# A two-block transformer on one core: seven-product pairs from the third pair of feed-forward tiles, sums one pair sooner

## The chip, the cores and the metric

One core of a Trainium2 chip runs the whole program in one launch. The metric is the device time of that launch in microseconds, the median of several runs. The engines are TensorE (PE, matmuls; PEld is its loading of weights), VectorE (DVE), ScalarE (ACT), GpSimd (POOL) and SyncE (SP, which issues most DMAs).

## The reference

Two blocks are applied to 512 tokens of width 1024, all in float32. The first is a hybrid of stick-breaking attention and a state-space scan. The second is: feed-forward part 1, a mixer (retention, multiscale pooling, gates), feed-forward part 2, a last norm. The change touches both feed-forward parts, which compute

```python
def swiglu_ffn(x, w_in, w_out):
    gate, up = jnp.split(x @ w_in, 2, axis=-1)
    return (jax.nn.silu(gate) * up) @ w_out
h = h + FFN_RES_WEIGHT * swiglu_ffn(rmsnorm(h, norm_ffn1[l]), ffn1_w_in[l], ffn1_w_out[l])
```

with 1024 inputs, an inner width of 2816 (`w_in` is 1024 x 5632, gate and up side by side) and a residual weight of one half.

## The kernel before, in words

Activations lie transposed: features on the 128 partitions, the 512 tokens along the free dimension, so an activation of width 1024 is 8 tiles of 128x512. To get float32 accuracy every operand is split into a rounded high part and the remainder (`split`, lines 111 to 118: ACT casts the high part, DVE subtracts). A product then takes three matmuls, high by high, high by low, low by high (`mm3`, lines with L102).

The inner width of 2816 is 22 tiles of 128, done in two halves of `FH` = 11. One step of the loop over `f` is a **pair**: the gate tile f and the up tile f. The result goes through Silu and the product of the two into `aa`. After each half come the eight output tiles.

There are two ways to do a pair. The **dense** one (f < `SF`, lines 1027 to 1048) takes for each of gate and up 8 blocks of weights by three matmuls of 512 columns, 48 matmuls. Its weights are loaded by SP (L131), cast by ACT (L137), and the low part is made by DVE (L139). The **seven-product** one (`strassen`, lines 976 to 1004) treats the pair as a 2x2 block product: inputs 0 to 3 and 4 to 7 (`xs`) by the two halves of the tokens, against gate and up weights. Seven products of 4 blocks by three matmuls of 256 columns, 84 matmuls (L959), are accumulated in the PSUM tiles `de`, `al`, `ga`. The order on PE is: `de` (opened ahead, before the pair before it is finished, by `open_pair`), then `al`, `ga`, `al`, `ga`, `al`, then the `de` of the next pair, then `al`. The second product into `al` follows a copy of the first out of it (ACT, L981). Besides the products it needs

- sums and differences of the activations, `T`, made once in each feed-forward part by four calls of `sums` (L902 to L905 on DVE, 128x256 each, then two splits: ACT L111, DVE L117). They read `xt`, the unsplit inputs. Every one of the four is needed by the second product (`ga`) of the first such pair;
- sums and differences of the weights, made for each pair by four calls of `prep`: part 0 splits the first loaded block (128x1024), parts 1 and 2 make two sums each (L939, L940, L943, L944 on DVE) and split them, part 3 casts half a block (ACT L111, L113) and gets its remainder by an accumulating DMA on POOL (L951). The raw blocks are loaded by `raws` (SP, L922).

In the first feed-forward part, `norm1` (called behind the last matmul of f=0) computes the norm's factors on DVE and POOL (L274 to L1105), broadcasts them by PE (`pb`), and rescales the eight residual tiles in place on DVE (L1110), which SP then writes to memory. In the second part `norm2` only makes one factor. The factor `Rb` is applied to the gate product on DVE (L1046), then Silu on ACT (L1047), the product with up on DVE (L1048) and the split into `aa`.

Order of work: on PE it is the order of the program, written out by hand. On the other engines the framework fixes an order ahead of the run, by its own planning. Working tiles (T before its split, the sums S, g, up, squares) come from one pool of 16 slots (`wk`), split activations from one of 54, weights' high parts from 4 slots (`wh`), low parts from 5 (`wl`), raw weights from 4 (`wr`), and PSUM tiles from 8.

In the kernel before, `SF` is 3: f = 0, 1, 2 are dense, the sums are made during f=1 (two) and f=2 (two), and the preparation of pair 3 during the up half of f=2.

Of the kernel before, what the change touches and what calls it, by code (L numbers as in the profile page):

```python
# [26 lines left out]
SLOTS = (54, 16, 4)  # L27
AHEAD = 3

SF = 3  # L30

PSH = (0, 1, 3, 5)
WARM = (12, 10, 4, 6, 6, 6)
# [20 lines left out]
def program(tc, A, out):  # L54
# [26 lines left out]
    def k_(dt=F32, name="k", shape=(P, S)):  # L81
        return wk.tile(list(shape), dt, tag="k", name=nm(name))
# [10 lines left out]
    def ps_(name="ps"):  # L93
        return pp.tile([P, S], F32, tag="p", name=nm(name))
# [9 lines left out]
    def mm3(o, w, x, start, stop):  # L104
        mm(o, w[0], x[0], start, False)
        mm(o, w[0], x[1], False, False)
        mm(o, w[1], x[0], False, stop)

    def cp(o, i, scale=None):
        if scale is None:  # L110
            ACT.copy(o, i)  # L111
        else:
            ACT.activation(o, i, AF.Copy, scale=scale)  # L113
# [6 lines left out]
    def split_into(h, l, src, scale=None):  # L120
        cp(h, src, scale)
        return lo(l, src, h, scale)
# [765 lines left out]
    def ffn(xs, xt, win, wout, norm, gnext, last=False, each=None):  # L888
# [7 lines left out]
        T = []  # L896

        def sums(k):

            t1, t2 = xt[k], xt[k + 4]  # L900
            u, v = k_(F32, "T"), k_(F32, "T")
            DVE.tensor_sub(u[:, lh], t1[:, rh], t1[:, lh])  # L902
            DVE.tensor_sub(u[:, rh], t2[:, rh], u[:, lh])
            DVE.tensor_sub(v[:, lh], t2[:, rh], t1[:, rh])
            DVE.tensor_sub(v[:, rh], t2[:, lh], u[:, rh])  # L905
            T.append((split(u, name="T"), split(v, name="T")))
# [11 lines left out]
        def raws(f):  # L918
            raw[f] = []
            for n in range(2):  # L920
                raw[f].append(wr.tile([P, 1024], F32, tag="wr", name=nm("wr")))
                SP.dma_start(raw[f][n], win[2 * f + n])  # L922

        def pair_of_tiles():
            return wh.tile([P, 1024], F32R, tag="wh", name=nm("wh")), wl.tile([P, 1024], F32R, tag="wl", name=nm("wl"))

        def quarter(i):
            return slice(512 * i, 512 * i + 512)

        def prep(f, part):  # L930
            r1, r2 = raw[f][:2]
            q0, q1 = quarter(0), quarter(1)
            h, l = pair_of_tiles()
            if part == 0:
                split_into(h, l, r1)
            elif part < 3:
                s, t = k_(F32, "S"), k_(F32, "S")
                if part == 1:
                    DVE.tensor_add(s, r2[:, q0], r2[:, q1])  # L939
                    DVE.tensor_sub(t, s, r1[:, q0])  # L940
                    raw[f].append(t)
                else:
                    DVE.tensor_sub(s, r1[:, q0], r2[:, q0])  # L943
                    DVE.tensor_sub(t, r1[:, q1], raw[f][2])  # L944
                for q, u in ((q0, s), (q1, t)):
                    split_into(h[:, q], l[:, q], u)
            else:

                cp(h[:, q0], r2[:, q1])
                cp(l[:, q0], r2[:, q1], -1.0)  # L950
                POOL.dma_start(l[:, q0], win[2 * f + 1, :, 512:1024], accum_op=ALU.add)  # L951
            ops.setdefault(f, []).append((h, l))
# [11 lines left out]
        def open_pair(f):  # L964
            pend[f] = ps_("de")
            product(pend[f], f, 0, 1, X(4, lh), True)
# [9 lines left out]
        def strassen(f, nf, aa, between):  # L976

            de, al, ga = pend.pop(f), ps_("al"), ps_("ga")
            g, v = k_(F32, "g"), k_(F32, "up")
            product(al, f, 0, 0, X(0, lh), True)  # L980
            ACT.copy(g[:, lh], al[:, lh])  # L981
            DVE.tensor_add(g[:, lh], de[:, lh], g[:, lh])
            if nf is not None:
                prep(nf, 0)
            product(ga, f, 1, 0, TT(0, lh), True)
            ACT.copy(v[:, rh], ga[:, lh])
            product(al, f, 1, 1, TT(0, rh), False)
            ACT.copy(g[:, rh], al[:, lh])
            if nf is not None:
                prep(nf, 1)  # L990
            product(ga, f, 2, 1, X(4, rh), False)
            DVE.tensor_add(g[:, rh], ga[:, lh], g[:, rh])
            product(al, f, 2, 0, TT(1, lh), False)
            order = DVE.tensor_add(v[:, rh], al[:, lh], v[:, rh])
            if nf is not None:
                prep(nf, 2)
                open_pair(nf)
            else:
                between()
            product(al, f, 3, 0, TT(1, rh), False)  # L1000
            finish(g, (al[:, lh], v[:, rh]), aa, order)
            if nf is not None:
                prep(nf, 3)
            ops.pop(f), raw.pop(f)

        for half in range(2):
            aa = []
            pos = []

            def opening():  # L1010

                pos.append(ps_("mp"))
                for k in range(2):
                    mm3(pos[0], so.next(), aa[k], k == 0, False)

            for f in range(half * FH, half * FH + FH):
                if f >= SF:
                    end = f == half * FH + FH - 1
                    if not end and f + 1 not in raw:
                        raws(f + 1)  # L1020
                    if end:
                        so.load(so.i)
                    strassen(f, None if end else f + 1, aa, opening)
                    if not end and f + 2 < half * FH + FH:
                        raws(f + 2)
                    continue
                pg, pu = ps_("mp"), ps_("mp")
                for n, ps in enumerate((pg, pu)):
                    for k in range(KD):
                        mm3(ps, si.next(), xs[k], k == 0, k == KD - 1)  # L1030
                        if each is not None and f == n == 0:
                            each(k)
                        if f == 0 and n == 1 and k in (2, 7):
                            norm(k // 7)
                        if f > 0 and n == 0 and k in (1, 5) and len(T) < 4:
                            sums(len(T))
                        if f == SF - 1 and n == 1 and k in (0, 2):
                            if k == 0:
                                raws(SF)
                            prep(SF, k // 2)  # L1040
                g = k_(F32, "g")
                if f == SF - 1:
                    prep(SF, 2)
                    open_pair(SF)
                    prep(SF, 3)
                DVE.tensor_mul(g, pg, ff["Rb"])  # L1046
                ACT.activation(g, g, AF.Silu)  # L1047
                DVE.tensor_mul(g, g, pu)  # L1048
                aa.append(split(g, name="aa"))
            for m in range(8):  # L1050
                if last and half == 1 and m == 6:
                    for i in (6, 7):
                        res[i] = a(F32, "res")
                        SP.dma_start(res[i], resd[i])
                    return aa, so
                xr = a(F32, "res") if last and half == 1 else tbl()
                SP.dma_start(xr, resd[m])
                k0 = 0 if m else 2
                ps = ps_("mp") if m else pos[0]
                for k in range(k0, FH):  # L1060
                    mm3(ps, so.next(), aa[k], k == 0, k == FH - 1)
                    if half == 0 and m == 7 and k in (0, 3, 4, 10):
                        if k == 0:
                            raws(FH)
                        else:
                            prep(FH, {3: 0, 4: 1, 10: 2}[k])
                if half == 0 and m == 7:
                    open_pair(FH)
                    prep(FH, 3)
                t = k_(F32, "t")  # L1070
                DVE.scalar_tensor_tensor(t, ps, 0.5, ff["Rb"], op0=ALU.mult, op1=ALU.mult)
                DVE.tensor_add(xr, xr, t)
                if half == 0:
                    SP.dma_start(resd[m], xr)
                    continue
                if gnext is not None:
                    nxt.append(split(xr, V(gnext, m), name="xs"))
                    SP.dma_start(resd[m], xr)
                else:
                    res[m] = xr  # L1080
                ff["ssq"] = accum(ff["ssq"], square(xr), DVE if m >= (4 if last else 6) else POOL)
# [451 lines left out]
```

## Time and profile before

| | us |
|---|---|
| median of 3 runs | 1715.0 (1714.86 to 1717.87) |
| the profiled execution | 1715.66 |
| its span | 1714.0 |
| PE busy | 1693.9 (99%) |
| DVE busy | 1112.6 (65%) |
| ACT busy | 807.9 (47%) |
| POOL busy | 221.0 (13%) |
| mean granted clock of PE | 0.992 |

The span runs from the first to the last instruction; the execution's time has a little around it. Rows of a timeline read: start, duration, engine, line of the kernel, operation, output tile and input tiles, count, and in brackets how long the engine had waited for nothing else and which instruction released it. A duration holds a part that overlaps with the next instruction, so the cost of one in a full queue is the distance from its start to the next start. In the chain of waits, each row is a stretch of the chain that ended last: start, length, what ran, how many. The first feed-forward part begins at about 515 us of the span, the second at about 1353.

### The profile page before, as it was taken

What the parts mean: (1) busy time and instruction counts of PE and PEld (TensorE: products, weight loads), DVE (VectorE), ACT (ScalarE), POOL (GpSimd) and SP (SyncE); (2) the same over time, 40 slices, a digit from 0 to 9 for tenths busy, and PEclk for the clock granted to TensorE, in tenths of its full rate; (3) what the DMA queues carried; (4) which work ended last, traced back from release to release, by engine and by line L of the source; (5) the groups of instructions that cost most, each with busy time, mean ns of one, the idle gap of its engine ahead of it and who ended that gap; (6) DMA issues with size and microseconds to landing.
All of it is one profiled execution on the core that took longest, in us unless ns stands there. A gap on an engine that the chain in (4) does not pass through costs nothing.

```text
span 1714.0 us, 24768 instructions
## 1 busy us (share of the span) xinstructions
PE 1693.9 (99%) x9488; PEld 1482.5 (86%) x9488; DVE 1112.6 (65%) x1757; ACT 807.9 (47%) x1344; POOL 221.0 (13%) x292
## 2 busy tenths in 40 slices
PE   9999899999999999999999999999999999999998
PEld 7898678888888998999888888888888899889987
DVE  7846953777957984798544636763544589559953
ACT  3555544777745661466333333332433466336642
POOL 0002202555400100000100000220000100000001
PEclk9999989999999999999999999999999999999999
DMA  9345448989563455445442322233333434544441
GB/s 327 106 127 187 137 128 220 215 192 210 146 153 107 125 155 164 129 125 155 164 150 91 88 91 86 80 99 97 93 95 129 158 93 124 166 129 137 124 166 50
DMA packets 84059, 236.36 MB, mean 138 GB/s; under 512 B 10018, under 2 KB 10338, under 8 KB 83940
## 3 DMA queue, kind: packets, MB, share of 16 engines
q1 hardware_dynamic: 74580, 210.66, 38.7%
q0 software_dynamic: 9360, 24.12, 8.2%
q8 instruction: 74, 1.21, 0.3%
q14 instruction: 45, 0.37, 0.1%
HBM read 207.44 MB, written 14.71 MB: 130 GB/s over the span
## 4 chain that ended last, share of the span: by engine, by line
PE 88%; DVE 3%; DMA 3%; issue 2%; ACT 2%; POOL 1%; SPq 0%; DVEq 0%; POOLq 0%; ACTq 0%
PE mp L102 53%; PE al L959 12%; PE mb L102 7%; PE ga L959 6%; PE de L959 3%; DMA wa<-in_adagt 1%; PE z L102 1%; PE sc L102 1%; PE po L102 1%; PE ro L102 1%; PE pw L772 1%; DMA wr<-in_wst 1%; DMA tb<-acd 1%; ACT tb L651 1%; ACT wh L137 0%
## 5 line engine op out<-in xcount | busy, mean ns | idle before, releaser
L137 ACT CAST wh<-wr 128x1024 fp32r<-128x1024 f32 (+3 forms) x212 | 217.6, 1030 | 463.7 <-PE mp L102 260.5
L139 DVE TENSOR_TENSOR wl<-wr,wh 128x1024 fp32r<-128x1024 f32 (+3 forms) x185 | 220.4, 1193 | 161.7 <-ACT wh L137 158.6
L102 PE MATMUL mp<-xsh,wh 128*128 128x512 f32 x416 | 164.6, 396 | 0.0
L102 PE MATMUL mp<-xsh,wl 128*128 128x512 f32 x416 | 162.2, 390 | 0.0
L102 PE MATMUL mp<-xsl,wh 128*128 128x512 f32 x416 | 162.0, 389 | 0.0
L111 ACT CAST wh<-S 128x512 fp32r<-128x512 f32 x152 | 93.7, 618 | 116.3 <-DVE S L943 59.2
L102 PE MATMUL mp<-aah,wh 128*128 128x512 f32 (+1 forms) x374 | 141.3, 378 | 0.0
L102 PE MATMUL mp<-aal,wh 128*128 128x512 f32 (+1 forms) x374 | 140.9, 377 | 0.0
L102 PE MATMUL mp<-aah,wl 128*128 128x512 f32 (+1 forms) x374 | 140.8, 376 | 0.0
L959 PE MATMUL al<-Th,wh 128*128 128x256 f32 x456 | 130.3, 286 | 2.3 <-ACT g L981 1.8
L959 PE MATMUL al<-Th,wl 128*128 128x256 f32 x456 | 129.0, 283 | 0.0
L959 PE MATMUL al<-Tl,wh 128*128 128x256 f32 x456 | 129.0, 283 | 0.0
L102 PE MATMUL mp<-hxh,wh 128*128 128x512 f32 x288 | 110.6, 407 | 2.0 <-ACT hxh L412 2.0
L102 PE MATMUL mp<-hxh,wl 128*128 128x512 f32 x288 | 107.0, 394 | 0.0
L102 PE MATMUL mp<-hxl,wh 128*128 128x512 f32 x288 | 106.7, 393 | 0.0
L117 DVE TENSOR_TENSOR wl<-S,wh 128x512 fp32r<-128x512 f32 x152 | 103.4, 684 | 0.2
L102 PEld LDWEIGHTS mp<-xsh,wl 128*128 128x128 f32 x416 | 78.0, 188 | 16.6
L102 PEld LDWEIGHTS mp<-xsh,wh 128*128 128x128 f32 x416 | 78.2, 188 | 15.7 <-issue 0.5
L102 PEld LDWEIGHTS mp<-xsl,wh 128*128 128x128 f32 x416 | 78.2, 188 | 15.6 <-issue 0.5
L959 PEld LDWEIGHTS al<-Th,wh 128*128 128x128 f32 x456 | 87.3, 192 | 4.2 <-ACT g L981 3.5
L959 PEld LDWEIGHTS al<-Tl,wh 128*128 128x128 f32 x456 | 87.4, 192 | 0.2
L959 PEld LDWEIGHTS al<-Th,wl 128*128 128x128 f32 x456 | 87.4, 192 | 0.0
(367 smaller groups left out, 4409.5 us busy)
## 6 DMA issues: line engine op xcount, KB each, us to landing
wr<-in_f1i SPq DMA_DIRECT2D x44, 512.0 KB, 3.9
wr<-in_f2i SPq DMA_DIRECT2D x44, 512.0 KB, 3.9
wr<-in_w2g SPq DMA_DIRECT2D x24, 512.0 KB, 3.5
wr<-in_f1o SPq DMA_DIRECT2D x22, 512.0 KB, 3.6
wr<-in_f2o SPq DMA_DIRECT2D x22, 512.0 KB, 3.6
tb<-res SPq DMA_DIRECT2D x32, 256.0 KB, 2.7
wr<-in_w2qk SPq DMA_DIRECT2D x16, 512.0 KB, 3.5
res<-res SPq DMA_DIRECT2D x24, 256.0 KB, 4.1
```

Of the source, the lines that this page charges most:

```text
L102: PE.matmul(o, l, r, start=start, stop=stop)
L111: ACT.copy(o, i)
L117: return DVE.tensor_sub(l, src, h.bitcast(F32))
L137: ACT.copy(h[:, :n], r[:, :n])
L139: DVE.tensor_sub(l[:, :n], r[:, :n], h[:, :n].bitcast(F32))
L651: ACT.activation(t[:, h, :], t[:, h, :], AF.Exp, bias=nac[:, hc : hc + 1])
L772: PE.transpose(pt[:, cc : cc + P], w[qb][:, kb * P : kb * P + P], ident)
L959: PE.matmul(o[:, lh], wk_[p], x[k][q], start=start and k == 0 and n == 0, stop=k == 3 and n == 2, skip_group_check=True)
```

## The change

`SF` becomes 2, so pair f=2 is done by seven products in both feed-forward parts, and the steps that lead up to the first such pair move one pair ahead. Of the four sums the first is called in the up half of f=0 behind the sixth block (k=5, ahead of the norm's call at k=7), the other three in the gate half of f=1 (k = 0, 3, 6). The loads of pair 2's raw blocks and the first two parts of its preparation are called in the up half of f=1, now at k = 0 and 3 in place of 0 and 2; the third and fourth part and `open_pair` follow behind f=1.

```diff
-SF = 3
+SF = 2
...
-                        if f > 0 and n == 0 and k in (1, 5) and len(T) < 4:
+                        if (f, n, k) in ((0, 1, 5), (1, 0, 0), (1, 0, 3), (1, 0, 6)):
                             sums(len(T))
-                        if f == SF - 1 and n == 1 and k in (0, 2):
+                        if f == SF - 1 and n == 1 and k in (0, 3):
                             if k == 0:
                                 raws(SF)
-                            prep(SF, k // 2)
+                            prep(SF, k // 3)
```

## The prediction

> **What bounds the kernel now.** I read the page first, then the chain of waits around both transitions from dense to seven-product pairs, then VectorE's (DVE's) and ScalarE's (ACT's) timelines there. The page says that TensorE (PE) is the bound.
>
> ```profile
> span 1714.0 us, 24768 instructions
> PE 1693.9 (99%) x9488; PEld 1482.5 (86%) x9488; DVE 1112.6 (65%) x1757; ACT 807.9 (47%) x1344; POOL 221.0 (13%) x292
> ```
>
> With PE at 99% a change counts only if it shortens PE's own work or the few places where PE waits. The chain of waits of the first feed-forward part (FFN 1) shows the two kinds of pair and such a place:
>
> ```profile
> 534.25 21.81 PE mp L102 x96
> 556.07 1.43 PE de L959 x12
> ...
> 561.83 1.69 PE al L959 x12
> ...
> 566.40 1.44 PE de L959 x12
> ...
> 572.52 1.69 PE al L959 x12
> ...
> 577.10 1.44 PE de L959 x12
> ...
> 587.18 1.44 PE de L959 x12
> ```
>
> Two dense pairs (f=1, 2) take 21.81 us, so 10.90 each; a seven-product pair in steady state takes 10.08 (577.10 to 587.18), 1.44 a product. The first one (f=3) is late: from its opening product `de` to the next `de` lie six products, 8.64 us, but 566.40 - 556.07 = 10.33. PE lost 1.69 there, and 577.10 - 566.40 - 10.08 = 0.62 in the next pair.
>
> What is late at 561.83, from the timelines of ACT and PE:
>
> ```profile
> 558.90 1.05 ACT L111 CAST wh<-wr 128x1024 fp32r<-128x1024 f32 x1 [0.85 <-ACT wh L111]
> ...
> 560.37 0.63 ACT L113 ACTIVATE wl<-wr 128x512 fp32r<-128x512 f32 x1
> 560.91 0.61 ACT L1047 ACTIVATE g<-g 128x512 f32<-128x512 f32 x1
> 561.43 0.35 ACT L981 COPY g<-al 128x256 f32<-128x256 f32 x1
> 561.83 0.38 PE L959 MATMUL al<-Th,wh 128*128 128x256 f32 x1 [1.45 <-ACT g L981]
> ```
>
> The third product writes `al` again, so it waits for ACT's copy out of `al` (L981). That copy stands in ACT's queue behind the Silu (L1047) of the last dense pair, and that waits for DVE's L1046. DVE is what is late:
>
> ```profile
> 526.98 0.16 DVE L274 TENSOR_SCALAR R1t<-pc 128x4 f32<-128x4 f32 x1 [8.65 <-PE pc L1091]
> ...
> 531.39 1.22 DVE L139 TENSOR_TENSOR wl<-wr,wh 128x1024 fp32r<-128x1024 f32 x1
> 533.46 1.23 DVE L139 TENSOR_TENSOR wl<-wr,wh 128x1024 fp32r<-128x1024 f32 x1 [0.85 <-ACT wh L137]
> 534.61 5.35 DVE L1110 SCALAR_TENSOR_TENSOR res<-res,vec,pb 128x512 f32<-128x512 f32 x8
> 539.87 0.68 DVE L1046 TENSOR_TENSOR g<-mp,tb 128x512 f32<-128x512 f32 x1
> 540.47 0.41 DVE L902 TENSOR_TENSOR T<-xt 128x256 f32<-128x256 f32 x1
> ...
> 548.36 0.68 DVE L117 TENSOR_TENSOR Tl<-T,Th 128x512 fp32r<-128x512 f32 x1
> 548.96 0.41 DVE L905 TENSOR_TENSOR T<-xt,T 128x256 f32<-128x256 f32 x1
> 549.30 0.68 DVE L117 TENSOR_TENSOR aal<-g,aah 128x512 fp32r<-128x512 f32 x1
> ...
> 553.05 1.22 DVE L117 TENSOR_TENSOR wl<-wr,wh 128x1024 fp32r<-128x1024 f32 x1
> 554.19 0.68 DVE L117 TENSOR_TENSOR Tl<-T,Th 128x512 fp32r<-128x512 f32 x1
> ...
> 556.71 1.29 DVE L117 TENSOR_TENSOR wl<-S,wh 128x512 fp32r<-128x512 f32 x2
> 557.92 0.68 DVE L944 TENSOR_TENSOR S<-wr,S 128x512 f32<-128x512 f32 x1
> ...
> 559.12 0.68 DVE L1046 TENSOR_TENSOR g<-mp,tb 128x512 f32<-128x512 f32 x1
> ```
>
> From 534.61 to 559.12 DVE runs without a pause: the eight rescalings of the residual (L1110), the products of f=0 and f=1, four sums with their splits, three parts of the preparation. The f=2 product L1046 comes last although its matmuls ended about 550.6. The order is that of the program within each pool of slots: tiles of the pool `wk` (T, S, g) are first written in program order. Hence the first sum starts right behind the first L1046, though DVE had idled 8.65 us before 526.98 and all of its inputs were there:
>
> ```profile
> 517.44 5.00 ACT L113 ACTIVATE xt<-res,gc 128x512 f32<-128x512 f32 x8
> ```
>
> FFN 2 has no L1110, and its DVE keeps up:
>
> ```profile
> 1365.34 21.81 PE mp L102 x96
> ...
> 1391.45 1.59 PE al L959 x12
> ```
>
> ```profile
> 1365.40 1.23 DVE L139 TENSOR_TENSOR wl<-wr,wh 128x1024 fp32r<-128x1024 f32 x1 [2.47 <-ACT wh L137]
> 1366.54 0.68 DVE L1046 TENSOR_TENSOR g<-mp,tb 128x512 f32<-128x512 f32 x1
> ...
> 1385.52 0.68 DVE L1046 TENSOR_TENSOR g<-mp,tb 128x512 f32<-128x512 f32 x1
> ```
>
> Unstalled, the third product would come at 1365.34 + 21.81 + 3 x 1.44 = 1391.47; it came at 1391.45 and was 0.15 long. PE lost 0.15 there.
>
> **The change, part by part.**
>
> *PE.* In each FFN pair f=2 goes from 48 matmuls of 512 columns to 84 of 256: 10.90 - 10.08 = 0.82 us less, 1.64 in both. That is all that PE can win by itself.
>
> *Loads.* Pair 2's two blocks of weights are loaded by L922 instead of L131, the same bytes from the same place at about the same place in SP's queue, into slots that come free as early as before: nothing. One accumulating DMA per FFN is added on POOL. Its cover now:
>
> ```profile
> 561.29 0.92 POOL L951 DMA_DIRECT2D wl<-in_f1i  x1 [31.34 <-DVE wl L117]
> ```
> ```profile
> wl<-in_f1i POOLq DMA_DIRECT2D x19, 256.0 KB, 5.3
> ```
>
> Landing at 561.29 + 5.3 = 566.6, it is 1.2 us ahead of its reader, the product behind `de` at 567.84 (566.40 + 1.44). DVE and ACT bring this step forward together with the product, so I cost it at nothing; if the 1.2 were gone, it would cost what is missing of them.
>
> *DVE and ACT.* Pair 2's transition stands one pair, 10.90 us, earlier on PE. What DVE does less ahead of the decisive L1046 (now that of f=1), by start-to-start times above: one sum, 4 x 0.34 + 2 x 0.60 = 2.56 (548.36 to 548.96 to 549.30), because the first sum is now written ahead of L274 and fits into the 8.65 us of idling behind the `xt` copies, which end at 522.44; the three operations of the middle dense pair (L1046, L1048, aal), 1.80; the first part of the preparation, 1.14 (553.05 to 554.19), which takes the place and the slots of the split at 531.39; and 0.26 since the split at 533.46 is gone and L1110 can start at 534.35, just behind the broadcasts that PE finished at 534.25. Together 5.76: L1046 at 559.12 - 5.76 = 553.36. The three other sums stay behind L1110 and the first L1046, by the order of the pool.
>
> From L1046 to the third product it was 561.83 - 559.12 = 2.71. The cast at 558.90 waited for a product and now waits for one much earlier, so the least is L1046, Silu and copy alone, 0.68 + 0.61 + 0.36 = 1.65. I take the middle, since other casts may still stand between: 555.5 (555.0 to 556.1). Equal to before would be 561.83 - 10.08 = 551.75. So FFN 1 gets **3.8 us longer** (3.3 to 4.3). Cross-check: PE could start this product at 534.25 + 10.90 + 4.32 = 549.47, so its stall grows from 1.45 to 6.0, and 6.0 - 1.45 - 0.82 = 3.8. Part of it falls on the second product, which needs all T and the first split at 556.71 (1.73 ahead of L1046): 551.65 against 548.03, 3.6 idle, 1.44 of work, then about 2.4 idle. The 0.62 in the next pair I leave as it is (0 to 1).
>
> FFN 2: L1046 comes 2.56 + 1.80 + 1.14 earlier, and 0.54 more: the split at 1365.40 is gone, so the first L1046 waits only for the broadcast (1365.34) and ACT's copy of it, some 0.6 like the 0.61 at 560.91. 1385.52 - 6.04 = 1379.48. The third product follows at 1381.15 at the least (1.65) and at 1383.24 at the most (2.71, and a cast of 1.05 as that at 558.90 in front). Equal to before is 1391.45 - 10.08 = 1381.37: -0.2 to +1.9. Without L1110 DVE is hardly behind, so I take the nearer end, **+0.5**.
>
> *Sum.* 3.8 + 0.5 = +4.3 us: the profiled execution's 1715.66 would be 1719.96. It stands 0.66 above the median of the runs, 1715.0, so **1719.3 us**.
>
> **The rivals.**
>
> *The clock drops as well.* PE has been throttled after gaps of this size:
>
> ```profile
> 189.95 1.12 PE L102 MATMUL pst<-xt,cbt 128*128 128x512 f32 x2 [2.49 <-DVE xt L644]
> 193.04 2.07 PE L102 MATMUL pst<-xt,cbt 128*128 128x512 f32 x2 [1.96 <-DVE xt L644]
> ```
> ```profile
> 191.00:195.00 4.00, 2.04 (x4) 0.61 0.21 84
> 195.00:199.00 4.00, 4.00 (x12) 0.53 0.01 2
> ```
>
> After 2.49 and 1.96 us of waiting the granted clock (the column behind the count) was 0.61 and 0.53 for 8 us: 4 x 0.39 + 4 x 0.47 = 3.4 us of PE's work lost at most. FFN 1's 3.6 and 2.4 are longer. Against it: part of the slow time lies in the second wait and is free. I price it at 2.5: 1721.8. [...]
>
> *L1110 goes behind the sums.* The eight rescalings serve only the residual's way out to memory. DVE is now free at about 532.5, and the first L1046 is ready a moment before the rescalings (its factor comes from the first broadcast). If the order lets the sums go ahead of them, the 534.61 to 539.87 = 5.26 us drop out: third product at 550.2, FFN 1 -1.5, with FFN 2 +0.5 1714.0, not slower than before. For it: that new idle moment. Against: before, such moments (0.85 ahead of 533.46, 2.47 ahead of 1365.40) were never given to sums. It decides as soon as a T row of f=1 starts ahead of L1110. If both stalls vanished altogether (1.69 + 0.62 + 0.15) it would be 1715.0 - 1.64 - 2.46 = 1710.9, the most that can be won.
>
> *The first sum stays behind L1046.* Then 2.56 is missing in both parts: 1719.3 + 5.1 = 1724.4. Against: its T tiles now precede L274's chain in the program.
>
> **How the numbers follow.** Run-to-run noise lets 0.2% (3.4 us) be told from no change, so the forecast is close to that bound. Forecast 0.36 (of it 0.25 over the bound, 0.11 under), clock 0.24, L1110 behind the sums 0.26 (0.05 of it over 0.2% faster), first sum late 0.07, small shifts that cancel 0.07 (0.01 faster). Slower: 0.25 + 0.24 + 0.07 = 0.56; faster 0.06; same 0.38. The range 1713.2 to 1723.6 takes in the case without the stall and the clock's, and leaves the late sum and the full gain outside; the likeliest case alone is 1718.1 (3.3 and -0.2) to 1721.2 (4.3 and 1.9).
>
> **What would show it.** T rows (L902 to L905) between 521 and 526.98; the last dense pair's L1046 near 553.4; idle PE rows of about 3.6 and 2.4 us behind L111/L117 and L981 near 548 to 555.5 in FFN 1, of at most 2.7 in FFN 2 near 1385; 20 accumulating DMAs per FFN in place of 19. Wrong if T rows of f=1 stand ahead of L1110, if ga's wait is absent, or if DVE's start-to-start times change; the clock's rival if windows near 552 to 560 show under 1.00.

## The result and the profile after

| | before | after |
|---|---|---|
| median, us | 1714.93 (4 runs, 1712.53 to 1717.87) | 1726.74 (4 runs, 1723.97 to 1728.43) |
| ratio of the times | | 1.0066 [1.0045, 1.0088] |
| the profiled execution | 1715.66 | 1725.76 |
| the same comparison repeated on another chip | 1715.96 (32 runs) | 1720.68 (9 runs), ratio 1.0043 [1.0023, 1.0063] |

The change makes the kernel slower: both intervals lie above 1. The forecast of 1719.3 was too low, and 1726.74 lies outside its range of 1713.2 to 1723.6. In the experiments below one of the ten runs with L1110 later and `SF` = 2 was slow, 2384.71 us at a mean granted clock of 0.651, and its row's ratio leaves it out.

Of the page of the changed kernel, the span and the busy times:

```profile
span 1724.1 us, 24962 instructions
PE 1698.4 (99%) x9560; PEld 1489.8 (86%) x9560; DVE 1122.5 (65%) x1779; ACT 813.8 (47%) x1360; POOL 222.1 (13%) x294
```

PE was to be busy 1.64 us less; it is busy 4.5 us more (1693.9 to 1698.4), a first sign that its matmuls ran slower somewhere. The span is 10.1 us longer. To place these I cut each execution at two events: VectorE's first operation of the norm (L274) and the first of the norm's small matmuls of FFN 2 (the tile `pc`). Of the changed kernel's timeline and chain:

```profile
529.60 0.16 DVE L274 TENSOR_SCALAR R1t<-pc 128x4 f32<-128x4 f32 x1 [8.31 <-PE pc L1091]
```
```profile
1368.86 0.79 PE pc L102 x8
```

and of the chain of the kernel before:

```profile
1360.12 0.79 PE pc L102 x8
```

| stage, us | before | after | difference |
|---|---|---|---|
| start to L274 (before the change acts) | 527.0 | 529.6 | +2.6 |
| FFN 1 and what follows, to `pc` of FFN 2 | 833.1 | 839.3 | +6.1 |
| FFN 2, to the end | 353.9 | 355.2 | +1.4 |

So the change costs **6.1 + 1.4 = 7.5 us** in its own two stages. The other 2.6 lie in a stretch where both kernels issue the same work but for one operation of a sum (520.87 below), which PE doesn't wait for there; the repetition below, where the same stretch is 3.9 shorter than before, speaks against the change as its cause.

**FFN 1.** VectorE's timeline of the changed kernel (here and below, 2.62 us are to be taken from a start in FFN 1 to compare it with before):

```profile
520.87 0.42 DVE L902 TENSOR_TENSOR T<-xt 128x256 f32<-128x256 f32 x1
...
531.20 0.42 DVE L903 TENSOR_TENSOR T<-xt,T 128x256 f32<-128x256 f32 x1
...
537.23 0.69 DVE L1046 TENSOR_TENSOR g<-mp,tb 128x512 f32<-128x512 f32 x1
537.83 5.35 DVE L1110 SCALAR_TENSOR_TENSOR res<-res,vec,pb 128x512 f32<-128x512 f32 x8
...
543.70 0.42 DVE L902 TENSOR_TENSOR T<-xt 128x256 f32<-128x256 f32 x1
...
556.15 0.69 DVE L1046 TENSOR_TENSOR g<-mp,tb 128x512 f32<-128x512 f32 x1
```

The second sum does stand behind L1046 of f=0 and the eight L1110, and L1046 of f=1 starts at 556.15 - 2.62 = 553.53, forecast 553.36. PE's timeline and then its chain:

```profile
552.79 0.57 PE L959 MATMUL ga<-Th,wh 128*128 128x256 f32 x1 [2.11 <-ACT wh L111]
...
553.89 0.58 PE L959 MATMUL ga<-Th,wl 128*128 128x256 f32 x1 [0.31 <-DVE wl L117]
...
558.51 0.58 PE L959 MATMUL al<-Th,wh 128*128 128x256 f32 x1 [2.12 <-ACT g L981]
```
```profile
558.51 2.93 PE al L959 x12
561.45 2.21 PE ga L959 x12
```

The third product starts at 558.51 - 2.62 = 555.89, forecast 555.5. But it then takes 2.93 and the fourth 2.21, in place of 1.44 each: 1.49 + 0.77 = 2.26 lost. The windows of PE show a lowered clock at this time (the columns: length, PE busy and its instructions, granted clock, DMA share, GB/s):

```profile
552.00:554.00 2.00, 0.90 (x3) 0.71 0.00 0
554.00:556.00 2.00, 2.00 (x10) 0.50 0.00 0
...
558.00:560.00 2.00, 1.49 (x7) 0.50 0.88 195
560.00:562.00 2.00, 2.00 (x11) 0.50 0.99 260
562.00:564.00 2.00, 2.00 (x15) 0.73 0.33 55
```

From the end of the first wait the granted clock is at half, and it stays there until about 563. The second product (`ga`) is slowed as well, but that time falls into the wait behind it, which ends with ACT's copy. The rival of the clock came true on top of the forecast's stall.

**FFN 2.** The chain of the changed kernel (here 1368.86 - 1360.12 = 8.74 are to be taken off):

```profile
1385.00 1.43 PE de L959 x12
...
1390.40 1.70 PE al L959 x12
...
1395.28 1.44 PE de L959 x12
...
1405.36 1.44 PE de L959 x12
...
1409.11 0.52 ACT wh L111
...
1410.59 0.61 ACT aah L111
1411.20 0.28 ACT g L981
...
1411.53 1.69 PE al L959 x12
...
1416.10 1.44 PE de L959 x12
```

The first pair loses 1395.28 - 1385.00 - 8.64 = 1.64, against 1395.92 - 1387.14 - 8.64 = 0.14 before, so it is 1.64 - 0.14 - 0.82 = 0.68 late. The second pair takes its 10.08. The third takes 1416.10 - 1405.36 = 10.74: the copy L981 again comes late, behind casts of weights and the split of `aa` on ScalarE, and 0.66 is lost where the kernel before lost nothing. 0.68 + 0.66 = 1.34.

### The profile page after: what moved, and what is told of

The parts are those of the page before. It is cut to its first block, busy times and chain, and to the rows that moved or that the text cites. A ratio compares the mean times of both kernels' runs of the same rounds, so it can differ in the third digit from the quotient of the medians.

```text
span 1724.1 us, 24962 instructions
## 1 busy us (share of the span) xinstructions
PE 1698.4 (99%) x9560; PEld 1489.8 (86%) x9560; DVE 1122.5 (65%) x1779; ACT 813.8 (47%) x1360; POOL 222.1 (13%) x294
## 3 DMA queue, kind: packets, MB, share of 16 engines
q8 instruction: 75, 1.23, 0.3%
## 4 chain that ended last, share of the span: by engine, by line
PE 87%; DVE 5%; DMA 2%; issue 2%; ACT 2%; POOL 1%; SPq 0%; DVEq 0%; POOLq 0%; ACTq 0%
PE mp L102 51%; PE al L959 13%; PE mb L102 7%; PE ga L959 6%; PE de L959 3%; DMA wa<-in_adagt 1%; PE z L102 1%; PE sc L102 1%; PE po L102 1%; PE ro L102 1%; PE pw L772 1%; DMA tb<-acd 1%; ACT tb L651 1%; PE msh L102 0%; ACT wh L137 0%
## 5 line engine op out<-in xcount | busy, mean ns | idle before, releaser
L102 PE MATMUL mp<-xsh,wh 128*128 128x512 f32 x384 | 152.2, 396 | 0.0
L102 PE MATMUL mp<-xsh,wl 128*128 128x512 f32 x384 | 149.7, 390 | 0.0
L102 PE MATMUL mp<-xsl,wh 128*128 128x512 f32 x384 | 149.6, 389 | 0.0
L959 PE MATMUL al<-Th,wh 128*128 128x256 f32 x480 | 137.8, 287 | 4.4 <-ACT g L981 4.0
L959 PE MATMUL al<-Th,wl 128*128 128x256 f32 x480 | 136.3, 284 | 0.0
L959 PE MATMUL al<-Tl,wh 128*128 128x256 f32 x480 | 136.3, 284 | 0.0
L117 DVE TENSOR_TENSOR wl<-S,wh 128x512 fp32r<-128x512 f32 x160 | 108.9, 685 | 1.3 <-ACT wh L111 1.1
L102 PEld LDWEIGHTS mp<-xsh,wl 128*128 128x128 f32 x384 | 72.1, 188 | 15.3
L102 PEld LDWEIGHTS mp<-xsl,wh 128*128 128x128 f32 x384 | 72.3, 188 | 14.5 <-issue 0.5
L102 PEld LDWEIGHTS mp<-xsh,wh 128*128 128x128 f32 x384 | 72.2, 188 | 14.4 <-issue 0.5
```

Source lines behind the costliest of these rows:

```text
L102: PE.matmul(o, l, r, start=start, stop=stop)
L117: return DVE.tensor_sub(l, src, h.bitcast(F32))
L959: PE.matmul(o[:, lh], wk_[p], x[k][q], start=start and k == 0 and n == 0, stop=k == 3 and n == 2, skip_group_check=True)
```

## The experiments

Ten kernels were run. For each, the ratio is to the kernel before on the same chip; the stages are those of the table above, from its profiled execution.

| kernel | median, us (runs) | ratio | start to L274 | FFN 1 | FFN 2 |
|---|---|---|---|---|---|
| FFN 1 alone | 1724.02 (5) | 1.0040 [1.0025, 1.0055] | -3.6 | +6.8 | -0.1 |
| FFN 2 alone | 1714.41 (10) | 1.0000 [0.9991, 1.0010] | +0.7 | 0.0 | +1.3 |
| the change again | 1720.68 (9) | 1.0043 [1.0023, 1.0063] | -3.9 | +6.1 | +1.3 |
| PE kept busy | 1721.74 (10) | 1.0037 [1.0024, 1.0050] | +1.8 | +4.3 | +1.3 |
| L1110 later, SF = 2 | 1717.27 (10) | 1.0003 [0.9992, 1.0013] | +3.9 | -0.6 | +1.3 |
| L1110 later, SF = 3 | 1714.75 (12) | 0.9993 [0.9977, 1.0009] | +2.3 | -2.2 | +0.2 |
| slots of their own for T | 1716.71 (10) | 1.0022 [1.0005, 1.0039] | +1.5 | +3.6 | -0.3 |
| L1110 later, part 3 first, FFN 1 alone | 1714.22 (12) | 0.9995 [0.9981, 1.0010] | +0.5 | -1.4 | 0.0 |
| L1110 later, own slots | 1712.64 (12) | 0.9991 [0.9973, 1.0008] | +1.0 | -0.5 | -0.4 |
| the same, part 3 first | 1713.14 (12) | 0.9992 [0.9976, 1.0008] | +0.3 | -0.8 | -0.9 |

The medians of before beside them were 1715.86 (26 runs, 1710.37 to 1718.61; the first, second, fourth and fifth row), 1715.96 (32 runs, 1710.05 to 1721.34; the third and the sixth to eighth) and 1714.74 (23 runs; the last two).

**Each feed-forward part alone.** `SF` is 2 in one of the two parts and 3, with the schedule of before, in the other (`last` is FFN 2). For FFN 1 alone, and with 2 and 3 exchanged for FFN 2 alone:

```diff
+        SF = 3 if last else 2
...
-                        if (f, n, k) in ((0, 1, 5), (1, 0, 0), (1, 0, 3), (1, 0, 6)):
+                        if ((f, n, k) in ((0, 1, 5), (1, 0, 0), (1, 0, 3), (1, 0, 6))) if SF == 2 else (f > 0 and n == 0 and k in (1, 5) and len(T) < 4):
...
```

> The change in FFN 1 alone; FFN 2 keeps SF=3 and its old places of the sums. Theory (DVE's backlog and then the clock in FFN 1; what lies ahead of FFN 1 is the variation of runs): FFN 1 6.1 us longer than before (3.8 by the late third product, 2.3 by the lower clock), FFN 2 as before, FFN 1 starting where it starts in other runs: 1714.9 + 6.1 = 1721.0. Rival (the change also delays what lies ahead of FFN 1 by 2.6 us or more): 1723.6 or more, with FFN 1 starting at 517 or later.

> The change in FFN 2 alone. Theory: FFN 2 1.4 us longer than before (0.82 won, 1.6 and 0.7 lost at the first two pairs), no clock lost there, FFN 1 as before: 1716.3. Rival (a shift ahead of FFN 1 comes with every new plan): 1718.9 or more.

FFN 1 alone has all of the loss that the times can tell; FFN 2's +1.3 is seen in its stage and is too small for them. The stages add up within 0.6: 6.8 + 1.3 against 7.5. FFN 1 alone costs 0.7 more than in the changed kernel mostly because its products from the third on take 2.93, 2.56 and 1.67 in place of 2.93, 2.21 and 1.43, 0.59 more; an estimate from these times is that the low clock reached further into them. Its median, 1724.02, is 3 us above the expected one, although the start of its profiled execution came 3.6 sooner than before; that execution was the fastest of the five (1718.82), and no trace says where the others lost their time.

**The change again**, unaltered, on another chip.

> The changed kernel once more, for the size of the loss. Theory (its stages account for all: FFN 1 6.1, FFN 2 1.4): 7.5 us above the kernel before, 1723.4, FFN 1 taking 839.3 us from the norm's first operation to FFN 2's in place of 833.1, wherever FFN 1 starts. Rival (there is a further steady loss ahead of FFN 1, as 1726.7 against 1714.9 suggested): 11.8 above, 1727.7.

Its two stages repeat to 0.1 us (+6.1, +1.3); its median is 4.7 above before's, with 7.5 inside the interval (3.9 to 10.8). Its start does not repeat: 523.1 against 529.6 for the very same instructions. The windows of PE in the changed kernel's first and second profiled execution show one of the places:

```profile
220.00:225.00 5.00, 4.17 (x19) 0.67 0.62 208
225.00:230.00 5.00, 5.00 (x21) 0.50 0.28 102
230.00:235.00 5.00, 5.00 (x19) 0.80 0.50 160
```
```profile
220.00:225.00 5.00, 4.73 (x33) 1.00 0.55 156
225.00:230.00 5.00, 5.00 (x24) 1.00 0.59 199
230.00:235.00 5.00, 5.00 (x28) 1.00 0.27 74
```

In the first the clock fell and 4.17 x 0.33 + 5.00 x 0.50 + 5.00 x 0.20 = 4.9 us of PE's work were lost; in the second it did not. Over the twelve profiled executions the start lies between 523.1 and 530.9. The start does not go with the change: with three dense pairs in FFN 1 it lay at 527.0, 527.7 and 529.3, with two between 523.1 and 530.9. So of the 11.8 us between the first two medians the stages give 7.5 to the change, and some 4 are not seen to be its own: 7.5 of 1715 is 1.0044, just below the lower edge of the first interval and in the middle of the second.

**PE kept busy.** In the changed kernel, 16 matmuls behind the first product and 30 behind the second one of FFN 1's first such pair, into a PSUM tile that nobody reads. They fill PE's waits and compute nothing that is used:

```diff
             product(al, f, 0, 0, X(0, lh), True)
+            if f == SF and not last:
+                busy = ps_("busy")
+                for _ in range(16):
+                    mm(busy[:, lh], xs[0][0][:, 0:P], xs[0][0][:, lh], True, True)
...
             product(ga, f, 1, 0, TT(0, lh), True)
+            if f == SF and not last:
+                for _ in range(30):
+                    mm(busy[:, lh], xs[0][0][:, 0:P], xs[0][0][:, lh], True, True)
```

> The changed kernel, with 16 and 30 matmuls of no use (256 columns, own PSUM tile) put into PE's two waits of the first seven-product pair of FFN 1, 1.9 and 3.6 us of work where PE only waits. Theory (the low clock is the price of PE's idling): granted clock 1.00 throughout FFN 1's transition, third and fourth product 1.44 each in place of 2.93 and 2.21, FFN 1 3.8 us longer than before in place of 6.1: 2.3 us less than the changed kernel, about 1724.4. [...]

Its chain, with the third and fourth product, and its windows of PE:

```profile
554.50 3.60 PE busy L102 x30
558.10 1.44 PE al L959 x12
559.54 1.44 PE ga L959 x12
```
```profile
554.00:556.00 2.00, 2.00 (x19) 1.00 0.29 27
...
560.00:562.00 2.00, 2.00 (x19) 1.00 0.93 220
```

The products run at full clock, and FFN 1 costs +4.3 in place of +6.1. The second one still waits for a cast and a split, 0.18 and 0.59 us. The third starts right behind the 30 matmuls, 29.17 us after L274 against 28.91 in the changed kernel: they overran ACT's copy by about 0.26, which is part of the 4.3. So 1.8 (by the stages) to 2.26 (by the two products) of the loss is the clock, and about 4 is the stall itself. This rests on the stages; the ratios, 1.0037 and 1.0043, can't tell the two kernels apart.

**L1110 later.** The residual goes to memory unscaled, and each of its tiles is multiplied when FFN 1's first half reads it back. All that is computed stays. With `SF` = 2, and with `SF` = 3, the kernel before but for this:

```diff
-        R1b = bcast(R1)
+        ff["R1b"] = tbl()
+        ACT.copy(ff["R1b"], bcast(R1))
         for m in range(8):
-            DVE.scalar_tensor_tensor(res[m], res[m], V("gf", m), R1b, op0=ALU.mult, op1=ALU.mult)
             SP.dma_start(resd[m], res[m])
...
+                if half == 0 and not last:
+                    DVE.scalar_tensor_tensor(xr, xr, V("gf", m), ff["R1b"], op0=ALU.mult, op1=ALU.mult)
                 DVE.tensor_add(xr, xr, t)
```

> The changed kernel, with the eight rescalings of the residual (L1110) taken out of DVE's queue behind the norm: the residual goes to memory unscaled and is scaled in the loop of output tiles, where it is read back. Theory (L1110's 5.26 us stand ahead of all that the first seven-product pair needs): third product 5.3 us earlier, no lower clock, FFN 1 about 1.2 us shorter than before in place of 6.1 longer, FFN 2 1.4 longer: 7.3 us less than the changed kernel, about 1719.4 (1715.1 if the shift ahead of FFN 1 is chance). Rival (the sums' own chain through ACT and the pool's order sets the pace, not L1110): third product moves by less than 2 us, clock still falls, 1724 or more.

> The kernel before (three dense pairs) with the rescalings (L1110) moved into the loop of output tiles. Theory (they are what makes the first seven-product pair late there too): the stalls of 1.69 and 0.62 go, FFN 1 about 2.0 us shorter, 1713.9. Rival (with three dense pairs the stall comes from ACT's order, not from DVE): FFN 1 within 0.5 us of before, 1715.9.

With the eight operations out of the queue, FFN 1's loss is gone (-0.6 in place of +6.1), and the granted clock is 1.00 in the windows from 548 to 564 us. But the pair's own 0.82 is not all there, and neither is the 2.31 that the kernel before lost in FFN 1, since other waits end last. PE's timeline with `SF` = 2, and the chain:

```profile
554.17 0.39 PE L959 MATMUL al<-Th,wh 128*128 128x256 f32 x1 [0.78 <-ACT g L981]
561.00 0.39 PE L959 MATMUL al<-Th,wl 128*128 128x256 f32 x1 [0.28 <-DMA wl<-in_f1i]
```
```profile
553.65 7.31 DMA wl<-in_f1i
```

The first pair, from `de` to `de`, loses 1.32, most of it in front of the third product. The second loses 0.54: the accumulating DMA, costed at nothing for its 1.2 us of cover, is now late, since the products come sooner and it took 7.31 against the median of 5.3. The fourth loses 0.67 as the third does in the changed kernel's FFN 2, behind casts on ScalarE. 2.31 + 0.82 - 1.32 - 0.54 - 0.67 = 0.60, as the stage has it. With `SF` = 3 the same edit takes away all but 0.14 of the stall of the kernel before. Its chain, from one `de` to the next:

```profile
558.37 1.43 PE de L959 x12
...
567.15 1.44 PE de L959 x12
...
577.23 1.44 PE de L959 x12
```

8.78 and 10.08, where before had 10.33 and 10.70: 1.55 + 0.62 = 2.2, as the stage has it. So in this stage three dense pairs (-2.2) are still better than two (-0.6).

**Slots of their own for T.** The claim that the pool's order, and not the engine's load, holds the other sums behind the first L1046 and L1110. In the changed kernel T gets four slots that no other tile uses, and the pool `wk` is cut from 16 to 12:

```diff
-SLOTS = (54, 16, 4)
+SLOTS = (54, 12, 4)
...
-            u, v = k_(F32, "T"), k_(F32, "T")
+            u, v = (wk.tile([P, S], F32, tag="T", name=nm("T"), bufs=4) for _ in range(2))
```

> The changed kernel, with the sums' tiles T in four slots of their own (12 left for the other working tiles). Theory (the order of the common pool kept the sums behind the first L1046 and so behind L1110): sums two and three run ahead of L1110 in DVE's idle time, the third product of FFN 1 comes about 2.4 us earlier, FFN 1 at most 3.7 us longer than before in place of 6.1, 1721.0. Rival (the sums stay behind L1110 for another reason): FFN 1 6.1 longer, 1723.4.

VectorE's timeline shows the second sum and most of the third in front of L1110:

```profile
535.97 0.42 DVE L902 TENSOR_TENSOR T<-xt 128x256 f32<-128x256 f32 x1
...
538.11 5.35 DVE L1110 SCALAR_TENSOR_TENSOR res<-res,vec,pb 128x512 f32<-128x512 f32 x8
543.38 0.68 DVE L1046 TENSOR_TENSOR g<-mp,tb 128x512 f32<-128x512 f32 x1
...
551.05 0.42 DVE L902 TENSOR_TENSOR T<-xt 128x256 f32<-128x256 f32 x1
```

This bears the claim out, with the reserve that the pool's size was changed with it. It is worth 2.5 in FFN 1 (+6.1 to +3.6) and 1.6 in FFN 2 (+1.3 to -0.3). Of the 2.5, 1.95 are the earlier start of the third product, where 2.4 was expected; the rest is a shorter slow time, which came here too: its third and fourth product take 2.56 and 1.89 in place of 2.93 and 2.21. The four slots hold two sums, so the fourth sum is now the last one (551.05), and the second product waits for that.

**Both, and part 3 of the preparation first.** The second and third product read what part 1 prepares, the fourth and fifth what part 2 does, and the last one, behind the next pair's `de`, what part 3 does, with the accumulating DMA. So that this DMA starts sooner, `prep(SF, 3)` is called ahead of `prep(SF, 2)`. It was run with the change in FFN 1 alone and L1110 later, and with the change in both parts, L1110 later and the slots, beside that kernel without it:

```diff
-            ops.setdefault(f, []).append((h, l))
+            ops.setdefault(f, {})[part] = (h, l)
...
+                    prep(SF, 3)
                     prep(SF, 2)
                     open_pair(SF)
-                    prep(SF, 3)
```

The third expectation below speaks of the order of the sums. The edit of that kernel is the one above, in both parts, and leaves the sums' calls as they are, so no run here tests their order.

> The change in FFN 1 alone, rescalings moved into the loop of output tiles, and the fourth part of the first pair's preparation (two casts and the accumulating DMA) called ahead of its third part. Theory (with L1110 gone, what is left in FFN 1 is that DMA, 7.3 us from issue to its reader, and 0.8 at the third product): seventh product no longer waits for the DMA, FFN 1 about 2 us shorter than before, 1713.8. Rival (the order of calls does not move ACT's casts): FFN 1 0.6 shorter, 1715.3.

> This keeps the third pair as the start of the seven products, multiplies by gf*R1b (L1110) later, inside the loop over tiles of half 0 of FFN 1, and gives the sums' tiles T four slots of their own. Theory: the copies L1110 and the pool's order are the only two things that hold the sums back; with both gone the 0.82 of each FFN is realised, FFN 1 is about 3 us shorter than before (late_sf2 was 0.6 shorter), FFN 2 0.3 to 0.8 shorter, about 1712. Rival: VectorE still owes the sums' splits and the transfer of the residual is still late, as in late_p3_ffn1: FFN 1 no more than 1.4 to 2.2 shorter than before, 1713.5 or more.

> As late_tpool, and the third sum of activations is made ahead of the second in FFN 1, since the third product reads it first. Theory: whatever wait is left at the third product in late_tpool goes; FFN 1 3 us or more shorter than before, 1712 or less. Rival: the wait only moves to the next product that reads a sum; FFN 1 as in late_tpool within 0.5.

With part 3 first in FFN 1 alone, no product waits for the DMA any more, as expected, and FFN 1 is 1.4 shorter, between the expected 2 and the rival's 0.6. The theory that L1110 and the pool's order are all that holds the sums back falls: with both out FFN 1 is -0.5 and -0.8, not -3. VectorE's timeline with both out:

```profile
545.28 0.42 DVE L902 TENSOR_TENSOR T<-xt 128x256 f32<-128x256 f32 x1
...
549.03 0.68 DVE L117 TENSOR_TENSOR Tl<-T,Th 128x512 fp32r<-128x512 f32 x1
549.63 0.68 DVE L1046 TENSOR_TENSOR g<-mp,tb 128x512 f32<-128x512 f32 x1
```

and PE's third product there:

```profile
552.23 0.39 PE L959 MATMUL al<-Th,wh 128*128 128x256 f32 x1 [1.57 <-ACT g L981]
```

The sums, their splits and the preparation still fill VectorE up to L1046, the same copy L981 still ends last, now with a cast of 128x1024 in front of it as well, and 1.57 is lost there. With part 3 first, L1046 comes 6 us sooner (543.36), but the copy then stands behind the cast of `aa`, for which VectorE is late with L1048 (549.51), and 1.23 is lost. In each of the three kernels a later pair loses 0.66 to 0.74 more, behind casts on ScalarE. The medians of these three lie below before's, but each interval contains 1: no version here is shown to beat the kernel before.

## Why the prediction was wrong

- **PE's 1.64 less:** right as a count. Nothing of it reached the end, as forecast.
- **The first sum into VectorE's idling:** right in its worth, wrong in its place. Of its four T operations one stands at 520.87; the others come between the norm's operations from 531.20, and the splits behind those. The wait of 8.31 in front of L274 stayed nearly whole. But all of the sum stands ahead of L1110, which starts at 537.83 - 2.62 = 535.21, 0.86 later than forecast; 0.60 of this is L1046 of f=0, now in front of it in place of behind. So of the 5.76 only the 0.26 for an earlier L1110 did not come, and L1046 of f=1 was 0.17 from its forecast.
- **Three sums behind L1110 and the first L1046, by the pool's order:** right; the rows show it, and T's own slots lift it. The rival that L1110 goes behind the sums did not happen in the changed kernel; only the first sum went ahead of it.
- **FFN 1's stall, +3.8:** right in its end. The third product started 0.4 later than forecast (555.89 against 555.5), inside the bounds, and the stall without the clock is about 4.0 by the kept-busy kernel (4.3 less 0.26). Its parts were not as forecast: the second product came at 552.79 - 2.62 = 550.17, not 551.65, and the waits were 2.11, 0.31 and 2.12, not 3.6 and 2.4, with the slowed second product filling what was left.
- **The clock, priced at 2.5 and left out of the sum:** this is the step that failed, the largest part of what the changed stages took beyond the forecast (7.5 against 4.3; of the 3.2, about 2.1 is the clock, 0.9 FFN 2 and 0.2 the stall). It was made a rival at 0.24 on the argument that part of the slow time lies in the second wait. Part of it did, and the price had allowed for that: 2.26 by the chain, 1.8 by the experiment. What was wrong was the likelihood. The rows quoted there (waits of 2.49 and 1.96, then 0.61 and 0.53) already had a lowered clock behind two waits of this size, and the forecast itself had a longer pair of them. In the changed kernel the granted clock was 0.50 for about 10 us (552.8 to 563.1); in the repetition and in FFN 1 alone the third and fourth product took 2.93 and 2.15, and 2.93 and 2.56, in place of 1.44.
- **FFN 2, +0.5:** mis-sized; measured +1.3 to +1.4. The first pair came out near it (+0.68). The other 0.66 are a wait in the third pair that the working did not look for: I followed VectorE's queue to the first pair and took ScalarE's for settled behind it.
- **The accumulating DMA at nothing:** right in the changed kernel, where no product waits for it. The condition, that the 1.2 us of cover stay, matters as written: in the kernel with L1110 later it was gone and the DMA ended last.
- **The range:** its bounds were those of the changed stages, with no term for the start, which differs by 8 us between profiled executions. By its stages the change gives 1715.66 + 7.5 - 0.66 = 1722.5, inside the range, as is the repetition's 1720.68. The first median, 1726.74, lies 4.2 above that: 2.6 is the start of the profiled execution, and 1.6 is how far the two profiled executions lie from their medians, which no trace places.

## What to carry to other kernels

When a forecast ends in two stalls of about two microseconds in front of the matmul engine, price the lowered clock into the sum, since this profile's own rows had shown it after stalls no longer (0.61 and 0.53 behind 2.49 and 1.96 us). Moving work one step earlier on the bound engine asks what the feeding engines still owe at that moment: here 24 us of VectorE's work without a pause stood ahead of the transition, and the 0.82 us a pair was lost to it. Where a comparison of two kernels differs by well under one per cent, cut the profiled executions into stages and see whether the difference lies where the code differs before explaining all of it.

## What the runs showed of the hardware

- Behind one wait of 2.11 us the clock was lowered in the changed kernel's FFN 1: the first matmul behind it (552.79) took 0.57, where the first behind a wait of 1.45 in the kernel before (561.83) took 0.38 at a clock of 1.00. The granted clock was 0.50 from about 552.8 to 563.1, some 10 us, with a second wait of 2.12 between. In the repetition the waits were 2.09 and 2.12, and the matmuls took 0.41 in place of 0.28 from 546.69 to 556.05.
- In these runs the length of the longest wait does not tell it alone. The clock was 1.00 behind the wait of 1.09 in the changed kernel's FFN 2 (1390.40). In the run with own slots for T, PE waited 0.79, 0.81, 0.48 and 1.10 between 550.2 and 554.93, each less than the 1.45 that the kernel before passed at 1.00, and its matmuls took 0.41 in place of 0.28 from 555.66 to 558.44.
- The same program lost 5 us or nothing at the same place in its first 240 us, by the granted clock (220 to 235 us above). PE idled 2.09 us of the 10 from 215 to 225 in the execution that lost them, and 2.48 in the other.
